# A hybrid encoder step on one Trainium2 core: the selection rounds' share of streamed work, and the engine of the first head pair's copies

## The chip, the cores and the metric

The kernel runs as one program on one core of a Trainium2 chip. The metric is the time of one execution on the device in microseconds (us); the number to predict is the median of the changed kernel's runs. A core has five engines that run unsynchronized except for semaphores: TensorE (matmuls, PE in the profile; its weight loads are PEld), VectorE (DVE), ScalarE (ACT), GpSimd (POOL) and SyncE (SP, which here mostly issues DMAs). Each engine takes its own instructions strictly in order: an instruction that waits holds up everything that stands behind it on that engine.

## The reference, cut to what matters

One layer of a streaming encoder for 1024 prompt tokens and 32 sample tokens. The normalized input `h` is projected once, and the columns are split; then come a state-space branch, a sparse attention branch, gates and an output projection.

```python
z = jnp.einsum('btd,de->bte', h, w_in)                      # h: 1056 x 1024
u, zs, q, k, v, za, qi, ki, wi, gm = jnp.split(z, offs, axis=-1)
...
logits = jnp.einsum('bthd,bsd->bths', qi, ki_all) * IDX_DIM ** -0.5
score = jnp.einsum('bth,bths->bts', wi, jax.nn.relu(logits))  # per query and key
score = jnp.where(adm[None, None, :], score, -jnp.inf)
top_val, top_idx = lax.top_k(score, n_sel)                    # 256 keys per query (136 for the sample)
kg, vg = gather(k_all, top_idx), gather(v_all, top_idx)
p = jax.nn.softmax(jnp.einsum('bthd,btkhd->bthk', q, kg) * HEAD_DIM ** -0.5)
o = jnp.einsum('bthk,btkhd->bthd', p, vg)                     # 8 heads of 64
```

Keys and values are outputs too, with one row per token (`k_p`, `v_p` for the prompt, `k_s`, `v_s` for the sample).

## The kernel before, in words

**Precision and tiles.** Each fp32 product is three TensorE matmuls of a high and a low part (`mm3`, lines 272 to 274: high by high, high by low, low by high). Activations stand transposed, 128 channels by 1056 tokens, in three chunks of 352 tokens.

**The stream.** All projections are `Job`s of 128 output columns in one queue `Z` (class `Stream`). A job has three chunks (0, 1, 2), a chunk eight steps, a step one `mm3`, so three matmuls of 352 columns. The stream is written into the program between other work: `run(us)` emits as many steps as `us` divided by 0.483 (with the rest carried over as credit), and `Z.after(us, f)` emits `f` that many steps later. A chunk's evacuation from PSUM is emitted `Z.lag` behind its last step; in the selection the lag is `LAG`, 4.0. So the numbers given to `run` do not wait for anything: they decide only where in each engine's order the instructions stand.

**PSUM in the selection.** Of each job, chunks 0 and 1 are the halves of one wide tile (tag `s`, named `pss` in the profile, two buffers) and chunk 2 has a narrow one (tag `z`, named `pz`, two buffers). Transposes go to `pt`, two buffers as well.

**The selection.** For each query the 256 largest scores are found by bisection of a threshold, one bit in each of 32 rounds (the loop over `b`, here called round 0 to 31). In a round VectorE counts three score tiles (line 1552), ScalarE counts four others (line 1550), then VectorE compares the counts and sets the next threshold for both (lines 1608, 1615, 1601). Between the counts and the comparison stands `run(RS)`: the round's share of the stream. In the stretch the stream holds the jobs K0, V0, Q0 (keys, values, queries of the first pair of heads), the merge gates g7 to g15, and za0 to za3. The gates' evacuation is a tanh on ScalarE (line 707). After the rounds VectorE marks the selected keys (`mark`), and the stream goes on by `run` with other shares until za3 is done. Then comes the attention, whose items alternate with steps of the stream.

**What K0 and V0 need.** `Heads(p, heng, eng)` builds the jobs of head pair `p`; `heng` splits their weights, and `eng` makes these copies: the three evacuations of K (line 1300) and of V (line 1304) into `zf`, and in `tok_major`, after transposes on TensorE, three copies into the token-major tile `tm` (line 1258 twice, four token blocks each; line 1261 once, the last 32 rows). `tm` has one buffer for keys and values together:

```python
tm = ap_.tile([128, 9, 128], F32, name="tm", bufs=1)
...
if b < 2:
    cp(eng)(tm[:, 4 * b:4 * b + 4].rearrange("p k c -> p (k c)"), pt)
    Z.after(TW if wide[0] else TK, lambda: part(b + 1))
else:
    cp(eng)(tm[:32, 8], pt[:32, 0:128])
    sp.dma_start(outp, tm[:, 0:8])
    sp.dma_start(outs, tm[:32, 8])
```

Pairs 1 to 3 (`HD[1:]`) are built with ScalarE as `eng`; their copies stand in the attention.

**Orders.** Inside `manual_schedule` each engine's order is the order of the program text as it is emitted; nothing is reordered later on VectorE and ScalarE there, nor on TensorE.

Of the kernel before, what the change touches and what calls it, by code (L numbers as in the profile page):

```python
# [36 lines left out]
TF, TK, TW = 1.5, 1.0, 4.5  # L37
FI = 0.0006
KA, LA = 5.0, 1.0
LAG, RS, MS, RM, RB = 4.0, 4.0, 0.008, 14.0, 1  # L40
FA, FF, SW, SA, SB = ((2.0, 1.3), (2.0, 1.3), (2.4, 1.6), (1.5, 1.5)), 0.08, 1.2, 4.0, 1.0
YR = 3.9, 2.0, 2.0, 8.0, 3.0
MR, ML, YS, YW, HI, HG, JO, SF = (), 1, 10, 15, 0, 0, 8, (2, 2, 2, 1)
# [16 lines left out]
def body(nc, tc, I, O, dbg=None):  # L60
# [3 lines left out]
    te, ve, se, ge, sp = nc.tensor, nc.vector, nc.scalar, nc.gpsimd, nc.sync  # L64
# [257 lines left out]
    now, ve = ve, Later(ve, todo)  # L322
# [190 lines left out]
    ve = now  # L513
# [753 lines left out]

    def khead(X, e, leng, gap=0, then=None):
        kH, kL = (ap_.tile([128, T], F32R, name=f"{n}{e}", bufs=1) for n in ("kH", "kL"))
        X.kH[e], X.kL[e] = kH, kL  # L1270

        def load(b):
            c = slice(512 * b, 512 * b + 512)
            kd = ap_.tile([128, 512], F32, name="kd", bufs=1)
            for hf_ in range(2):
                sp.dma_start(kd[64 * hf_:64 * hf_ + 64], X.kd[64 * e:64 * e + 64, c])

            def parts():
                split(kH[:, c], kL[:, c], kd, ve, leng)
                if b == 0:  # L1280
                    load(1)
                elif then:
                    then()
            if gap:
                Z.after(gap, parts)
            else:
                parts()
        load(0)
# [120 lines left out]

    def attention(p, X):  # L1410

# [19 lines left out]
        class Sample(Soft):  # L1431
            e, i = -1, 4

            def scores(self):
                self.products(64, 544, mb8, X.qsm.rearrange("p e q -> p (e q)"), (X.kall,))

# [10 lines left out]
            def out(self):  # L1447
                po = ps_x("po", 1)
                for k in range(5):
                    n = 128 if k < 4 else 32  # L1450
                    te.matmul(po[:, 0:64], X.cvt[:, k] if k < 4 else X.vts, self.PS[:n, k], start=k == 0, stop=k == 4)
                for e in range(2):
# [101 lines left out]

    wide[0] = True
    Z.lag = LAG
    X = Heads(0, ge, ve)

    def q0_end():
        Z.after(1.0, lambda: X.values(0))  # L1560
# [355 lines left out]
```

## Time and profile before

| | us |
|---|---|
| median of the runs | 1037.23 |
| lowest of the runs | 1037.08 |
| the profiled execution | 1032.88 |
| its span, first to last instruction | 1031.1 |
| outside the span | 1.78 |
| TensorE busy | 984.4 |
| VectorE busy | 765.8 |
| ScalarE busy | 530.8 |
| GpSimd busy | 232.2 |

The profiled execution is one of its own, 4.35 us under the median. All rows come from it, with times from the start of the span. Busy time counts instructions that compute; waiting and issuing of DMAs do not count. TensorE's matmuls are pipelined, so the rows of two of them overlap; a step's three matmuls start 0.48 us apart from the next step's.

### The profile page before, as it was taken

To read this page: it belongs to the slowest core of one execution; us is meant where nothing else is said; L and a number is where in the kernel's file an instruction comes from. 1 tells how busy PE (TensorE), PEld (TensorE's weight loads), DVE (VectorE), ACT (ScalarE), POOL (GpSimd) and SP (SyncE) were. 2 spreads that over 40 slices of the span, in tenths; PEclk is the share of its full clock that TensorE was granted. 3 is DMA by queue.
4 is the path that set the end of the run, shared out by engine and by line. 5 is a ranking of instruction groups with operands and counts; after the bars stand their busy time and mean duration, and the time that the engine had idled before them with its cause. 6 is when DMAs were issued, how large, how long until landed. Compare 5 with 4: busy or idle time off the path is not lost.

```text
span 1031.1 us, 17149 instructions
## 1 busy us (share of the span) xinstructions
PE 984.4 (95%) x6194; PEld 920.7 (89%) x6194; DVE 765.8 (74%) x1760; ACT 530.8 (51%) x1153; POOL 232.2 (23%) x459
## 2 busy tenths in 40 slices
PE   5999999999999999899999999999999999999997
PEld 3799999999998889899899999889998988998786
DVE  4669798996857879999999556667558776785544
ACT  3642245546545665778883356465466554343111
POOL 3102400000010023242333523324412222430000
PEclk9999999999999999999999999999999999999999
DMA  9922522327672213333222522232226523753311
GB/s 306 283 74 84 162 68 65 96 74 242 196 222 83 62 31 94 94 93 95 83 84 85 171 90 63 73 94 63 97 59 192 161 76 113 247 167 122 133 62 62
DMA packets 124177, 121.68 MB, mean 118 GB/s; under 512 B 14272, under 2 KB 104852, under 8 KB 124092
## 3 DMA queue, kind: packets, MB, share of 16 engines
q1 hardware_dynamic: 122544, 119.69, 37.6%
q8 instruction: 49, 0.80, 0.3%
q10 hardware_dynamic: 1388, 0.86, 0.3%
q14 instruction: 36, 0.29, 0.1%
q0 software_dynamic: 160, 0.03, 0.0%
HBM read 85.64 MB, written 34.34 MB: 116 GB/s over the span
## 4 chain that ended last, share of the span: by engine, by line
PE 77%; DVE 10%; ACT 6%; issue 3%; DMA 3%; SPq 0%; POOL 0%; POOLq 0%; ACTq 0%; DVEq 0%
PE pz L272 12%; PE pz L273 12%; PE pz L274 12%; PE pss L272 3%; PE pss L274 3%; PE pss L273 3%; DVE junk L1552 3%; PE pss L1386 3%; PE psm L1885 3%; PE psm L1886 3%; PE psm L1887 3%; DMA wm<-in_w_mod 2%; PE pt L1479 2%; PE pspo L1498 2%; PE pss L1215 2%
## 5 line engine op out<-in xcount | busy, mean ns | idle before, releaser
L272 PE MATMUL pz<-hH,wh 128*128 128x352 f32 (+1 forms) x776 | 260.5, 336 | 0.4 <-DVE qis L1060 0.4
L274 PE MATMUL pz<-hH,wl 128*128 128x352 f32 (+1 forms) x776 | 250.7, 323 | 0.0
L273 PE MATMUL pz<-hL,wh 128*128 128x352 f32 (+1 forms) x776 | 250.6, 323 | 0.0
L265 POOL TENSOR_TENSOR wl<-raw,wh 128x256 fp32r<-128x256 f32 (+1 forms) x184 | 130.9, 739 | 111.6 <-ACT wh L260 111.3
L272 PEld LDWEIGHTS pz<-hH,wh 128*128 128x128 f32 (+1 forms) x776 | 145.2, 187 | 4.0 <-issue 0.8
L273 PEld LDWEIGHTS pz<-hL,wh 128*128 128x128 f32 (+1 forms) x776 | 145.3, 187 | 1.5
L274 PEld LDWEIGHTS pz<-hH,wl 128*128 128x128 f32 (+1 forms) x776 | 145.0, 187 | 0.4
L1550 ACT ACTIVATE junkb<-sco,thr 128x768 bf16<-128x768 f32 (+3 forms) x128 | 96.8, 756 | 36.6 <-DVE thr L1615 26.6
L1552 DVE TENSOR_SCALAR_CACHE_REDUCE junk<-sco,thr 128x1024 bf16<-128x1024 f32 (+2 forms) x96 | 105.4, 1098 | 2.2
L272 PE MATMUL pss<-hH,wh 128*128 128x352 f32 x304 | 101.5, 334 | 5.8 <-POOL wh L264 3.2
L273 PE MATMUL pss<-hL,wh 128*128 128x352 f32 x304 | 99.8, 328 | 0.2 <-DVE hL L74 0.2
L274 PE MATMUL pss<-hH,wl 128*128 128x352 f32 x304 | 99.7, 328 | 0.0
L264 POOL CAST wh<-raw 128x256 fp32r<-128x256 f32 x92 | 36.2, 433 | 189.0 <-PE pz L273 178.1
L1482 DVE TENSOR_TENSOR PL<-pt,PH 128x512 fp32r<-128x512 f32 (+2 forms) x96 | 50.3, 552 | 25.8 <-ACT PH L1481 22.9
L1481 ACT CAST PH<-pt 128x512 fp32r<-128x512 f32 (+2 forms) x96 | 42.9, 482 | 46.3 <-PE pt L1479 44.5
L272 PEld LDWEIGHTS pss<-hH,wh 128*128 128x128 f32 x304 | 58.6, 193 | 8.9 <-POOL wh L264 4.9
L273 PEld LDWEIGHTS pss<-hL,wh 128*128 128x128 f32 x304 | 58.5, 192 | 0.5 <-DVE hL L74 0.4
L274 PEld LDWEIGHTS pss<-hH,wl 128*128 128x128 f32 x304 | 58.4, 192 | 0.2 <-POOL wl L265 0.2
L1223 DVE SCALAR_TENSOR_TENSOR sco<-rl,wi,sco 128x384 f32<-128x384 f32 (+6 forms) x49 | 45.5, 936 | 16.9 <-ACT rl L1218 16.3
L1218 ACT ACTIVATE rl<-pss 128x384 f32<-128x384 f32 (+6 forms) x56 | 41.2, 738 | 31.8 <-PE pss L1216 30.2
L1399 ACT ACTIVATE Sm<-Sm,mx 128x128 f32<-128x128 f32 (+8 forms) x68 | 52.7, 775 | 8.0 <-DVE mx L1392 7.3
L1392 DVE CUSTOM_DVE_ANT_0 Sm<-pss,mb 128x512 f32<-128x512 f32 (+4 forms) x68 | 40.2, 591 | 22.0 <-PE pss L1386 21.3
(408 smaller groups left out, 2210.2 us busy)
## 6 DMA issues: line engine op xcount, KB each, us to landing
raw<-in_w_in SPq DMA_DIRECT2D x44, 512.0 KB
thD<-tg SPq DMA_DIRECT2D x16, 528.0 KB
tgl<-thD SPq DMA_DIRECT2D x16, 528.0 KB
wm<-in_w_mod SPq DMA_DIRECT2D x8, 1024.0 KB
rraw<-in_w_mod SPq DMA_DIRECT2D x4, 1024.0 KB
kd<-kd SPq DMA_DIRECT2D x32, 128.0 KB
xo<-in_x_prompt SPq DMA_DIRECT2D x8, 512.0 KB
rawo<-in_w_o SPq DMA_DIRECT2D x8, 512.0 KB
```

The lines of the kernel that those rows point to most:

```text
L265: leng.tensor_sub(wl[:, c], raw[:, c], f32(wh[:, c]))
L272: te.matmul(ps, wh, xh, start=first, stop=False)
L273: te.matmul(ps, wh, xl, start=False, stop=False)
L274: te.matmul(ps, wl, xh, start=False, stop=last)
L1218: se.activation(rl[:m, :nk], ps[:m, :nk], AF.Relu)
L1223: ve.scalar_tensor_tensor(sco[i][:m, :nk], rl[:m, :nk], w, sco[i][:m, :nk], op0=ALU.mult, op1=ALU.add)
L1392: ve.tensor_tensor_reduce(self.P[:m, c], S, self.mask[:m, c], -0.125, 3.0e38 if a == 0 else mx[:m, 0:1], op0=ALU.add, op1=ALU.min, accum_o ...
L1399: se.activation(P, P, AF.Exp, scale=-1.0, bias=self.mx, accum_out=self.rs)
L1481: se.copy(PH[:, b0:b1_, oc], src)
L1482: ve.tensor_sub(PL[:, b0:b1_, oc], src, f32(PH[:, b0:b1_, oc]))
L1550: se.activation(junkb[:m, :nk], x[:m], AF.Sign, bias=t, accum_out=cnt[:m, k:k + 1])
L1552: ve.tensor_scalar(junk[:m, :nk], x[:m], t, None, op0=ALU.is_lt, op1=ALU.add, accum_out=cnt[:m, k:k + 1])
```

## The change

Two constants change. `RS`, the share of the stream that each of the 32 rounds hands out, goes from 4.0 to 4.1. The first head pair is built with ScalarE (`se`) in place of VectorE (`ve`) as `eng`, so its six evacuations and six token-major copies go to ScalarE.

```diff
-LAG, RS, MS, RM, RB = 4.0, 4.0, 0.008, 14.0, 1
+LAG, RS, MS, RM, RB = 4.0, 4.1, 0.008, 14.0, 1
...
     wide[0] = True
     Z.lag = LAG
-    X = Heads(0, ge, ve)
+    X = Heads(0, ge, se)
```

On ScalarE, rounds 5 to 7 of the selection (the four rows of line 1550 are one round's counts; `zf` is an evacuation, `tm` the token-major tile, `kall` the sample's keys). The difference, before (-) and after (+):

```order
+L1258 COPY tm<-pt 128x512
+L1304 COPY zf<-pss 128x352
+L1550 ACTIVATE junkb,cnt<-sco_3235,thr 128x768
+L1550 ACTIVATE junkb,cnt<-sco_3233,thr 128x512
+L1550 ACTIVATE junkb,cnt<-sco_3232,thr 128x384
+L1550 ACTIVATE junkb,cnt<-sco_3238,thr 32x544
+L1261 COPY tm<-pt 32x128
 L1338 COPY kall<-zf 128x32
+L1304 COPY zf<-pz 128x352
+L1258 COPY tm<-pt 128x512
 L1550 ACTIVATE junkb,cnt<-sco_3235,thr 128x768
```

Round 5 ends with K's second token copy and V's evacuation, round 6 with K's last 32 rows, the small key copy, V's last evacuation and V's first token copy; the last row shown is the first count of round 7. On VectorE V's first token copy stood in round 7.

On ScalarE, rounds 7 to 9, at the query casts (`qs`):

```order
 L1550 ACTIVATE junkb,cnt<-sco_3232,thr 128x384
 L1550 ACTIVATE junkb,cnt<-sco_3238,thr 32x544
+L1258 COPY tm<-pt 128x512
 L1316 CAST qs_4509<-pss 64x352
 L1316 CAST qs_4510<-pss 64x352
```

In round 8 V's second token copy stands ahead of the two casts; in round 9 its last 32 rows do in the same way.

On ScalarE, round 14, the evacuations of gate job g8 (`tg` out of `pss` is chunk 0 or 1, out of `pz` chunk 2):

```order
 L707 ACTIVATE tg<-pss 128x352
+L707 ACTIVATE tg<-pz 128x352
+L1550 ACTIVATE junkb,cnt<-sco_3235,thr 128x768
+L1550 ACTIVATE junkb,cnt<-sco_3233,thr 128x512
+L1550 ACTIVATE junkb,cnt<-sco_3232,thr 128x384
+L1550 ACTIVATE junkb,cnt<-sco_3238,thr 32x544
```

Chunk 2 now follows chunk 1 in the same round; before, a round's counts stood between them. Counted through the whole order, the rounds that hold the evacuation of chunk 1 are, before: g7 11, g8 14, g9 17, g10 20, g11 23, g12 25, g13 28, g14 31; after: 11, 14, 16, 19, 22, 25, 28, 30. On TensorE no instruction of the selection changes its place.

On TensorE, one of the places in the attention (`Sm` are softmax rows being transposed):

```order
 L274 MATMUL pz<-hH_81,wl 128x352
-L272 MATMUL pz<-hH_749,wh 128x352
-L273 MATMUL pz<-hL_750,wh 128x352
-L274 MATMUL pz<-hH_749,wl 128x352
 L1479 MATMUL pt<-idf,Sm 128x128 x2
+L272 MATMUL pz<-hH_749,wh 128x352
+L273 MATMUL pz<-hL_750,wh 128x352
+L274 MATMUL pz<-hH_749,wl 128x352
```

One step of the stream has moved from before two transposes to behind them.

## Rows read from the trace of the kernel before

**Rows 1.** Stretch, length, then busy us of PE, PEld, DVE, ACT, POOL (instructions).

```profile
385.00:540.00 155.00, 146.67 (x898) 144.17 (x891) 146.79 (x331) 117.37 (x282) 52.44 (x99) 0.98 0.30 92
...
586.00:870.00 284.00, 271.90 (x1816) 254.18 (x1816) 187.18 (x543) 162.57 (x377) 85.91 (x181) 1.00 0.32 97
```

**Rows 2.** Timeline of TensorE: start, duration, instruction, idle before it and releaser.

```profile
419.58 0.65 PE L1343 MATMUL pt<-idf,ckt 128*128 128x128 f32 x4 [0.49 <-DVE tm L1261]
424.39 0.75 PE L1256 MATMUL pt<-idf,zf 128*128 128x128 f32 x4 [2.22 <-DVE tm L1258]
...
464.64 0.40 PE L272 MATMUL pss<-hH,wh 128*128 128x352 f32 x1 [2.38 <-ACT tg L707]
479.04 0.40 PE L272 MATMUL pss<-hH,wh 128*128 128x352 f32 x1 [1.10 <-POOL wh L264]
...
504.70 0.40 PE L272 MATMUL pss<-hH,wh 128*128 128x352 f32 x1 [1.10 <-POOL wh L264]
...
527.82 0.32 PE L272 MATMUL pss<-hH,wh 128*128 128x352 f32 x1
```

**Rows 3.** Granted TensorE clock (before the last two numbers) behind the long spells.

```profile
424.75:428.25 3.50, 3.50 (x15) 3.50 (x14) 3.33 (x8) 2.44 (x6) 1.56 (x5) 0.51 0.00 0
466.00:469.00 3.00, 3.00 (x12) 3.00 (x11) 2.90 (x6) 1.84 (x5) 0.98 (x2) 0.50 0.51 133
```

**Rows 4.** Timeline of ScalarE: first counts of rounds 1, 7, 11, 12; evacuations; copies.

```profile
392.32 0.94 ACT L1550 ACTIVATE junkb<-sco,thr 128x768 bf16<-128x768 f32 x1 [5.83 <-DVE thr L1613]
...
420.32 0.94 ACT L1550 ACTIVATE junkb<-sco,thr 128x768 bf16<-128x768 f32 x1 [0.80 <-DVE thr L1615]
...
445.79 0.94 ACT L1550 ACTIVATE junkb<-sco,thr 128x768 bf16<-128x768 f32 x1 [2.17 <-DVE thr L1615]
...
449.20 0.44 ACT L707 ACTIVATE tg<-pss 128x352 f32<-128x352 f32 x1
449.78 0.94 ACT L1550 ACTIVATE junkb<-sco,thr 128x768 bf16<-128x768 f32 x1
...
478.46 0.44 ACT L707 ACTIVATE tg<-pss 128x352 f32<-128x352 f32 x1
...
525.78 0.44 ACT L707 ACTIVATE tg<-pss 128x352 f32<-128x352 f32 x1
...
610.72 0.58 ACT L1258 COPY tm<-pt 128x512 f32<-128x512 f32 x1
611.19 0.47 ACT L1304 COPY zf<-pz 128x352 f32<-128x352 f32 x1
```

**Rows 5.** Timeline of VectorE: threshold instructions of round 2, copies, waits.

```profile
400.42 0.48 DVE L1608 TENSOR_TENSOR keep<-cnt,lim 128x7 int32<-128x7 f32 x1
400.94 0.66 DVE L1615 SCALAR_TENSOR_TENSOR thr<-keep,nxt 128x7 int32<-128x7 int32 x1
...
409.24 0.68 DVE L1258 COPY tm<-pt 128x512 f32<-128x512 f32 x1
409.84 0.51 DVE L1304 COPY zf<-pss 128x352 f32<-128x352 f32 x1
...
419.25 0.28 DVE L1261 COPY tm<-pt 32x128 f32<-32x128 f32 x1
...
430.53 1.06 DVE L1320 TENSOR_TENSOR qs<-pss,qs 64x352 fp32r<-64x352 f32 x2 [0.18 <-ACT qs L1316]
...
470.82 0.17 DVE L1615 SCALAR_TENSOR_TENSOR thr<-keep,nxt 128x7 int32<-128x7 int32 x1
...
586.04 0.29 DVE L1392 CUSTOM_DVE_ANT_0 Sm<-pss,mb 128x128 f32<-128x128 f32 x1 [5.83 <-PE pss L1386]
```

**Rows 6.** Timeline of SyncE: K's rest, za3's 528 KB store, the load that waits for it.

```profile
419.55 0.35 SPq L1263 DMA_DIRECT2D out_k_s<-tm  x1
...
586.36 0.32 SPq L698 DMA_DIRECT2D zaD<-zt  x1
589.56 0.32 SPq L1417 DMA_DIRECT2D ya<-zaD  x1
```

## The prediction, made before the changed kernel ran

> **What bounds the kernel now.** I read the stretches first, then TensorE's idle spells, then what releases them. In the two stretches that the change touches (the selection from 385 to 540 us, the attention from 586 to 870) TensorE is busy 146.67 of 155.00 and 271.90 of 284.00 us [rows 1]; between them it does not idle at all. So only what TensorE waits for can be won. In the selection it idles six times: 0.49, 2.22, 2.38 us and three spells of 1.1 us, two of which are shown; 8.4 in all [rows 2]. After the two long ones its granted clock falls to 0.5, the lower of its two levels, for nearly all of a 3.5 us and a 3.0 us stretch [rows 3], which costs some 1.7 us each. All that could be gained here is therefore 8.4 + 3.4 = 11.8 us, 1.1%.
>
> What holds TensorE in those spells? The three of 1.1 us are put down to GpSimd's weight cast. But the spell that ends at 479.04 ends 0.14 us after ScalarE's tanh of 478.46 + 0.44 [rows 2, 4]. That fits the code: chunks 0 and 1 of a job share one of two wide PSUM tiles, so job j may start only when chunk 1 of job j-2 is evacuated, and ScalarE does that behind the counts of the round in which the planner put it. **TensorE's speed limit in the selection is the pace of the rounds**, not its own work. Two jobs without idle take 527.82 - 504.70 = 23.12 us, 11.56 each [rows 2]; three rounds take longer. The binding event near the end is the evacuation at 525.78 + 0.44 + 0.14 = 526.36, in round 28 (the first of the 32 is round 0), which job g15 waits for; it started at 527.82 [rows 2, 4]. From there to the attention nothing stops TensorE, and VectorE then waits 5.83 us for it [rows 5]. So I need one number: **how far does round 28 move?** If it ends d later, TensorE gains 527.82 - 526.36 - d = 1.46 - d us, provided that no wait remains behind it.
>
> **RS = 4.1.** A round hands out 8.49 steps instead of 8.28. TensorE's own order in the selection does not change; what changes is the round in which ScalarE finds an evacuation. The order shows g8's chunks 1 and 2 together in round 14, where g12's two stood in round 25 before. Chunk 1 of g9, g10, g11 and g14 is thus evacuated one round earlier (rounds 16, 19, 22, 30), some 4 us, which frees the three spells of 1.1 us. Chunk 1 of g8, g12 and g13 stays in rounds 14, 25 and 28. So TensorE runs ahead after g10, gains, and meets the wall again at round 25 (g14) and round 28 (g15). This is why the 3.2 us of extra quota (32 x 0.1) do not appear as such: the sum stops at 1.46 - d.
>
> **Twelve copies from VectorE to ScalarE.** Off VectorE go six evacuations of 0.51 us, four copies of 0.68 and two of 0.28 [rows 5], 6.3 us of instruction time, about 5.4 by the distance of their starts. But a round without a copy on VectorE is not VectorE's: from 445.79 to 449.78 ScalarE's counts fill 3.41 us, its tanh 0.44, and the next counts start 3.99 us after the first [rows 4]. ScalarE has 0.14 us of room. I lay out its rounds from 392.32, where round 1 starts [rows 4]:
> - rounds 1 and 3, counts and one evacuation: 3.99 each.
> - rounds 2 and 5: the same or slightly more on ScalarE, but GpSimd's weight split lies over the end of the round. In round 2 it stretched the two short threshold instructions to 0.48 and 0.66 us from 0.17 [rows 5], so 0.8 more: 4.79 each.
> - round 4: token copy and evacuation start 0.47 apart [rows 4], 3.41 + 0.47 + 0.47 = 4.35.
> - Round 6 starts at 392.32 + 21.91 = 414.23. It holds four copies: K's 32-row rest, the small key copy, V's last evacuation, and V's first token copy, which the order puts one round earlier than before.
>
> Here the change **adds a wait**. V's token tile is K's token tile (one buffer), so V's first copy must wait until K's rest has been stored to HBM, and that store is issued only after the rest is copied, in the same round. Before, the store went out at 419.55 [rows 6] and a whole set of counts lay in between. Now the rest is copied at 414.23 + 3.41 to 417.9, the store goes out, and ScalarE stands; behind V's copy in its queue are the counts of round 7, and behind those VectorE's threshold. No row shows this landing. From below it is hidden: the four copies alone give 3.41 + 0.2 + 0.12 + 0.36 + 0.59 = 4.68 us (the first three read from overlaps like those of rows 4, an estimate), so round 7 at 418.9. From above it is the 528 KB store of 586.36, whose reader was let go at 589.56 [rows 6], 3.2 us: round 7 at 417.9 + 3.2 + 0.6 = 421.7. The store is 16 KB, so nearly none of that time is data, but it cannot be nothing; I take the middle, 1.6 us: 420.1 against 420.32 before [rows 4]. So the whole relief of rounds 1 to 6 shrinks to 0.2 us.
>
> The Trainium skill (DMA: Bandwidth & Descriptors, Anatomy of one DMA) gives a transfer a fixed 2.0 us, most of it the receipt of the write; its fit is for GpSimd's path, this store goes by SyncE. By it round 7 would start at 420.5 and the gain at the end would be 0.4 us smaller. No run here shows the landing yet.
>
> Rounds 8 and 9: V's next copies stand ahead of the query casts. VectorE waits for both casts (it idled 0.18 us for them at 430.53, behind its own copy [rows 5]), so 0.47 and 0.20 us come onto the path; in round 7 the copy that leaves was inside such a wait and saves nothing. The value and key splits that move between rounds 9 to 12 keep their sum. So d = -0.2 + 0.47 + 0.20 = **0.5 us later**, and it stays to round 28 (the round with two evacuations costs the same in round 14 as in 25).
>
> **TensorE's early spells.** The 0.49 and 2.22 us waits for VectorE's token copies go: V's first copy is done by 420.1, and TensorE asks for that buffer at 424.39 - 2.22 - 0.49 = 421.7 [rows 2]. With the slow stretch behind them that is 4.4 us, but it is given back: job g9 would arrive at 462.26 - 11.56 - 4.4 = 446.3, and its PSUM tile comes free with round 11's evacuation at 449.20 + 0.44 + 0.14 + 0.5 = 450.3 [rows 2, 4]. I expect a new spell of about 4 us there, one of 1 to 2 us before g10 (round 14), none before g11 to g13, and about 1 us before g14 and g15.
>
> **Attention.** The stream enters it with another fraction of a step, so at some 40 places one step of three matmuls (0.48 us) stands on the other side of a transpose, score or product. TensorE idles 12.1 us there now [rows 1], in spells of 0.2 to 1.6 us. Both directions occur; I take 0, bounds -1.5 and +1.5.
>
> **Sum.** 1.46 - 0.5 = 1.0 us faster. Against the profiled execution, 1032.88 - 1.0 = 1031.9; it lies 4.35 us under the median, so the median becomes 1037.23 - 1.0 = **1036.2 us**. With the ends of the unknown landing, d runs from -0.7 (hidden) to +2.1 (3.2 us): 1035.1 to 1037.9; with the attention's 1.5, 1033.6 to 1039.4.
>
> **Rivals.**
> 1. *The relief counts in full.* If ScalarE has room (its copies overlap its counts, the landing is hidden) rounds end by the 5.4 us earlier that VectorE loses. For it: VectorE is busy 146.79 of 155.00 us and ScalarE 117.37 [rows 1]. Against it: the 0.14 us of room. Round 28 is then at 521.0, g15 starts there, gain 1.46 + 5.4 = 6.9: 1030.4.
> 2. *ScalarE becomes the bound, slower than before.* The landing takes the full 3.2 us, and V's value splits, now both in round 9, meet GpSimd's split for another 0.8: d = 2.1 + 0.8 = 2.9, loss 1.4: 1038.7. It decides from d = 1.46 on. For it: all the moved copies stand in ScalarE's queue in front of counts that VectorE's next threshold needs. Against it: a 16 KB store.
> 3. *The quota counts as it says*: 3.2 us more work under the rounds. That would need the wall of rounds 25 and 28 not to bind, for instance if TensorE arrives there late; then the three spells of 1.1 us and the clock stretch after 464.64 fall away, 3.2 + 1.7 = 4.9: 1032.3. Against it: g13's evacuation keeps its round.
> 4. *The attention's shifted steps* outweigh all, by 2 us or more in either direction: 1034 or 1039.
>
> **Chances.** Forecast 0.55, first rival 0.12, second 0.17, third 0.08, fourth 0.08. The range 1031.5 to 1039.5 leaves out the first rival and the outer parts of the second and fourth. About 2% (21 us) is what a measurement of this kernel tells from no change; no case comes near it: faster 0.01, same 0.98, slower 0.01.
>
> **What would show it.** In the changed profile: ScalarE idle before V's first token copy in round 6, released by a transfer; round 7 at about 420; round 11's tanh near 449.6; no idle of TensorE before 440, then a spell near 450 that ends with that tanh, a slow clock stretch after it, no spells of 1.1 us after g10; g15 at about 526.9; the scores of the attention 1 us earlier, with VectorE still waiting there. Wrong would be the whole if a round without copies on VectorE got shorter than 3.99 us, if ScalarE did not stand in round 6, or if TensorE's spells in the attention changed by more than 1.5 us.

## The result, and the profile after

The changed kernel takes 1028.94 us where the kernel before took 1035.71 in the same series (medians of 6 runs each): a ratio of 0.9945, 95% interval 0.9925 to 0.9966. One of the six runs of the kernel before, 1212.29 us, counts in its median but not in the ratio; the other five have a median of 1034.34 us. Timed once more beside three of the experiments the ratio was 0.9966 (0.9953 to 0.9979). Both intervals hold 0.9953 to 0.9966, a gain of 3.5 to 4.9 us. I had forecast a gain of 1.0 us, and a time of 1036.2 us in a range from 1031.5 to 1039.5; 1028.94 lies below it.

The profiled executions took 1032.88 us before and 1029.09 after. The windows of the changed kernel, with the columns of [rows 1]; the second one begins 0.6 us behind the attention's first scores, that of [rows 1] 0.3 us:

```profile
385.00:540.00 155.00, 147.85 (x911) 145.32 (x904) 140.50 (x320) 123.25 (x297) 52.32 (x99) 0.98 0.32 95
584.00:868.00 284.00, 274.33 (x1828) 255.65 (x1827) 187.16 (x544) 163.24 (x378) 85.48 (x180) 1.00 0.32 100
```

TensorE is 1.2 us busier in the selection and 2.4 us busier in the attention. The gain has two places, then, and the sum had put a small one in the first and nothing in the second.

TensorE's timeline after, the four waits of the selection and the attention's first scores (they answer to [rows 2]):

```profile
451.93 0.63 PE L272 MATMUL pss<-hH,wh 128*128 128x352 f32 x1 [5.54 <-ACT tg L707]
...
501.08 0.40 PE L272 MATMUL pss<-hH,wh 128*128 128x352 f32 x1 [0.50 <-ACT tg L707]
...
513.45 0.40 PE L272 MATMUL pss<-hH,wh 128*128 128x352 f32 x1 [0.59 <-ACT tg L707]
...
525.72 0.40 PE L272 MATMUL pss<-hH,wh 128*128 128x352 f32 x1 [0.51 <-ACT tg L707]
...
583.40 0.22 PE L1386 MATMUL pss<-kH,qs 128*128 128x128 f32 x1
```

The six spells have become one long one, where the prediction put it, and three of half a microsecond, all of which end with a tanh of ScalarE. Job g15 starts at 525.72 instead of 527.82. The tanh that frees it, in round 28, and the one that ends the long spell, in round 11:

```profile
451.35 0.44 ACT L707 ACTIVATE tg<-pss 128x352 f32<-128x352 f32 x1
...
525.14 0.44 ACT L707 ACTIVATE tg<-pss 128x352 f32<-128x352 f32 x1
```

525.14 + 0.44 + 0.14 = 525.72, to the digit. Behind the long spell the granted clock (third number from the end) is at its lower level for some four microseconds, as after the long spells of [rows 3]:

```profile
452.00:456.00 4.00, 4.00 (x14) 4.00 (x15) 3.86 (x9) 2.95 (x7) 0.00 (x0) 0.50 0.42 103
456.00:460.00 4.00, 4.00 (x25) 4.00 (x24) 3.74 (x10) 3.75 (x10) 0.00 (x0) 0.92 0.65 229
```

The wait that the change adds is there too. ScalarE in round 6, and the first count of round 7 (compare [rows 4]):

```profile
417.69 0.24 ACT L1261 COPY tm<-pt 32x128 f32<-32x128 f32 x1
417.84 0.21 ACT L1338 COPY kall<-zf 128x32 f32<-128x32 f32 x1
417.96 0.44 ACT L1304 COPY zf<-pz 128x352 f32<-128x352 f32 x1
420.95 0.59 ACT L1258 COPY tm<-pt 128x512 f32<-128x512 f32 x1 [2.55 <-DMA out_k_s<-tm]
421.43 0.94 ACT L1550 ACTIVATE junkb<-sco,thr 128x768 bf16<-128x768 f32 x1
```

The store that it waits for, on SyncE:

```profile
417.96 0.34 SPq L1263 DMA_DIRECT2D out_k_s<-tm  x1
```

It was issued at 417.96, and its tile was free at 420.95: 2.99 us.

**Where the rounds made it up.** I measure from round 1 (392.32 before, 392.49 after). Round 7 is 0.94 us later than before, round 9 1.77, round 15 0.28 *earlier*, round 28 0.82 earlier. So 2.05 us come back from round 9 to round 15 and 0.54 after that. In the kernel before, rounds 12 and 14, with the second and the fourth of the first pair's key splits (lines 73 and 74), read so on VectorE:

```profile
453.11 0.64 DVE L73 CAST kH<-kd 128x512 fp32r<-128x512 f32 x1
453.78 1.11 DVE L74 TENSOR_TENSOR kL<-kd,kH 128x512 fp32r<-128x512 f32 x1
454.82 0.69 DVE L1608 TENSOR_TENSOR keep<-cnt,lim 128x7 int32<-128x7 f32 x1
...
463.99 0.57 DVE L73 CAST kH<-kd 128x512 fp32r<-128x512 f32 x1
464.60 1.10 DVE L74 TENSOR_TENSOR kL<-kd,kH 128x512 fp32r<-128x512 f32 x1
465.62 0.70 DVE L1608 TENSOR_TENSOR keep<-cnt,lim 128x7 int32<-128x7 f32 x1
466.35 0.65 DVE L1615 SCALAR_TENSOR_TENSOR thr<-keep,nxt 128x7 int32<-128x7 int32 x1
```

and GpSimd beside them, in the kernel before, splits weights:

```profile
452.04 3.45 POOL L265 TENSOR_TENSOR wl<-raw,wh 128x256 fp32r<-128x256 f32 x4
...
463.56 3.42 POOL L265 TENSOR_TENSOR wl<-raw,wh 128x256 fp32r<-128x256 f32 x4
```

The same two key splits of the changed kernel, the second now in round 11, the fourth still in round 14, and then its GpSimd with the two weight splits around them:

```profile
451.43 0.42 DVE L73 CAST kH<-kd 128x512 fp32r<-128x512 f32 x1
451.89 0.69 DVE L74 TENSOR_TENSOR kL<-kd,kH 128x512 fp32r<-128x512 f32 x1
452.50 0.16 DVE L1608 TENSOR_TENSOR keep<-cnt,lim 128x7 int32<-128x7 f32 x1
...
465.12 0.42 DVE L73 CAST kH<-kd 128x512 fp32r<-128x512 f32 x1
465.58 0.69 DVE L74 TENSOR_TENSOR kL<-kd,kH 128x512 fp32r<-128x512 f32 x1
466.19 0.36 DVE L1608 TENSOR_TENSOR keep<-cnt,lim 128x7 int32<-128x7 f32 x1
466.58 0.31 DVE L1615 SCALAR_TENSOR_TENSOR thr<-keep,nxt 128x7 int32<-128x7 int32 x1
```

```profile
448.16 2.78 POOL L265 TENSOR_TENSOR wl<-raw,wh 128x256 fp32r<-128x256 f32 x4
465.75 1.82 POOL L264 CAST wh<-raw 128x256 fp32r<-128x256 f32 x4 [14.80 <-PE pz L273]
```

A split of weights may start when the job two places ahead of it has ended and left its buffers. Job g8 now ends earlier, since TensorE's early waits are gone, and g9 later, since it waits 5.54 us to start; so one split moved ahead of these key splits and the next mostly behind them. The second key split also stands one round earlier in VectorE's order, but that alone would not have freed it: counted from round 1, the two key splits now start at 58.9 and 72.6 us, and GpSimd's weight splits of the kernel before lay at 58.3 to 63.2 and 69.8 to 74.7 us. I added up by how much VectorE's instructions in rounds 9 to 14 exceed what they take beside an idle GpSimd: 3.2 us before, 1.2 after, and the difference is what came back there. Whether this is the cause, and not only what stands beside it, the experiments must tell.

### The profile page after: what moved, and what is told of

Read it like the earlier page. It is cut to its first block, busy times and chain, and to the rows that moved or that the text cites. A ratio compares the mean times of both kernels' runs of the same rounds, so it can differ in the third digit from the quotient of the medians.

```text
span 1027.3 us, 17151 instructions
## 1 busy us (share of the span) xinstructions
PE 984.7 (96%) x6194; PEld 920.5 (90%) x6194; DVE 759.5 (74%) x1748; ACT 536.3 (52%) x1165; POOL 232.1 (23%) x459
## 4 chain that ended last, share of the span: by engine, by line
PE 71%; DVE 11%; ACT 10%; issue 3%; DMA 3%; POOL 0%; SPq 0%; ACTq 0%; POOLq 0%; DVEq 0%
PE pz L272 12%; PE pz L273 11%; PE pz L274 11%; ACT junkb L1550 6%; DVE junk L1552 3%; PE pss L1386 3%; PE psm L1885 3%; PE psm L1886 3%; PE psm L1887 3%; DMA wm<-in_w_mod 2%; PE pt L1479 2%; PE pss L272 2%; PE pss L273 2%; PE pss L274 2%; PE pspo L1498 2%
## 5 line engine op out<-in xcount | busy, mean ns | idle before, releaser
L265 POOL TENSOR_TENSOR wl<-raw,wh 128x256 fp32r<-128x256 f32 (+1 forms) x184 | 128.4, 725 | 117.3 <-ACT wh L260 117.0
```

Of the source, the lines that this page charges most:

```text
L265: leng.tensor_sub(wl[:, c], raw[:, c], f32(wh[:, c]))
```

## The experiments

All ratios are to the kernel before on the same chip. **My theory**: the gain is the sum of two effects that the change does not name: the moved weight splits of GpSimd (some 2 us), and another order of steps in the attention (some 2 us). **The rivals**: the relief of VectorE as such; the quota as such.

| kernel | ratio (95%) | round 1 | first scores | end | round 1 to scores | scores to end |
|---|---|---|---|---|---|---|
| before | 1 | 392.32 | 585.66 | 1031.1 | 193.34 | 445.4 |
| changed | 0.9945 (0.9925 to 0.9966) | 392.49 | 583.40 | 1027.3 | 190.91 | 443.9 |
| after_again | 0.9966 (0.9953 to 0.9979) | 391.80 | 582.36 | 1026.3 | 190.56 | 443.9 |
| quota_alone | 0.9971 (0.9954 to 0.9988) | 392.43 | 584.18 | 1027.4 | 191.75 | 443.2 |
| scalar_alone | 1.0003 (0.9992 to 1.0014) | 393.23 | 585.55 | 1030.9 | 192.32 | 445.4 |
| both_old_fraction | 0.9981 (0.9967 to 0.9994) | 395.69 | 586.55 | 1032.0 | 190.86 | 445.4 |
| before_new_fraction | 0.9978 (0.9965 to 0.9992) | 392.65 | 586.20 | 1029.4 | 193.55 | 443.2 |
| before_no_splits | 0.998 (0.997 to 0.999) | 395.52 | 585.60 | 1031.0 | 190.08 | 445.4 |
| after_two_splits_more | 0.9996 (0.9985 to 1.0008) | 394.60 | 588.84 | 1032.6 | 194.24 | 443.8 |
| after_own_v_tile | 0.9949 (0.9936 to 0.9962) | 392.33 | 582.15 | 1025.7 | 189.82 | 443.6 |
| after_other_fraction | 1.0015 (1.0005 to 1.0025) | 392.98 | 584.35 | 1033.6 | 191.37 | 449.2 |
| own_v_tile_no_splits | 0.9899 (0.9879 to 0.992) | 391.63 | 576.68 | 1020.7 | 185.05 | 444.0 |
| quota_own_v_tile | 0.996 (0.9946 to 0.9975) | 395.89 | 586.49 | 1030.6 | 190.60 | 444.1 |
| own_v_tile_third_fraction | 0.9943 (0.9926 to 0.9959) | 394.18 | 584.23 | 1027.6 | 190.05 | 443.4 |
| own_v_tile_small_pieces | 0.9984 (0.9972 to 0.9995) | 394.75 | 588.39 | 1032.0 | 193.64 | 443.6 |
| own_v_tile_large_pieces | 0.9997 (0.9984 to 1.001) | 392.94 | 585.70 | 1029.3 | 192.76 | 443.6 |

The last two columns are worked out from the three before them, each from one profiled execution. They are the better measure of the parts, since the time up to round 1 differs from one execution to the next.

### The two halves of the diff

**quota_alone** takes RS = 4.1 alone, **scalar_alone** the twelve copies alone.

```diff
-    X = Heads(0, ge, se)
+    X = Heads(0, ge, ve)      # quota_alone, in the changed kernel
-    X = Heads(0, ge, ve)
+    X = Heads(0, ge, se)      # scalar_alone, in the kernel before
```

> Only RS = 4.1; the first heads' copies stay on VectorE. TensorE's order is that of the changed kernel, its attention included. Theory (my reading of the two traces): about 2 us of the gain come from the selection, where TensorE's long wait before g9 moved GpSimd's weight split off the two rounds (12 and 14) in which it stretched VectorE's key splits, so that the rounds made up the time they had lost; about 2 us come from the attention, whose steps of the stream stand on other sides of its transposes and scores. Here the waits of 0.49 and 2.22 us stay and nothing is moved off rounds 12 and 14, so round 28 ends where it did and g15 gains 0.5 to 1.5 us, the attention 2: 2.5 to 3.5 us faster, 1032.2 to 1033.2 against 1035.7. Rival 'the quota is all': the full 5.7 us, 1030. Rival 'ScalarE's relief is all': nothing, 1035.7.

> Only the twelve copies go to ScalarE; RS = 4.0. TensorE's order is that of the kernel before everywhere. Theory: the attention gains nothing; the early waits of TensorE go, a long one stands near g9 or g10, the weight split moves, and g15 starts 0 to 1 us earlier: 1034.7 to 1035.7. Rival 'the relief is all': 5 to 6 us faster, 1030. Rival 'ScalarE pays': 1 us slower, 1036.7, since V's first token copy waits 3 us for the store of K's rest and no quota makes up for it.

The copies alone have no gain that can be measured, so the rival that credits VectorE's relief falls, and with it the first rival of the prediction (5.4 us of relief). The quota alone cannot be told from the whole change: 0.9971 lies in the interval of the changed kernel's second timing, and from round 1 to the end its trace takes 635.0 us, those of the changed kernel 634.8 and 634.5, that of the kernel before 638.8. Both effects of my theory come with the quota, then; that the copies add anything to it is not shown.

My expectation for the quota fitted in size and was wrong on the way. I had TensorE's 2.22 us wait for V's token copy stay and nothing move off rounds 12 and 14. But the wait shrank to 0.84 us, a spell of 4.86 us came before g9, GpSimd's weight splits moved as in the changed kernel, and VectorE's excess in rounds 9 to 14 was 1.0 us.

The added wait shows where it comes from. With the quota alone, VectorE stands for the same store:

```profile
422.37 0.69 DVE L1258 COPY tm<-pt 128x512 f32<-128x512 f32 x1 [2.31 <-DMA out_k_s<-tm]
```

With the copies on ScalarE and RS = 4.0 nothing waits there: V's first copy stands one round later. So the wait belongs to the quota, not to the engine. For scalar_alone the trace shows a selection shorter by 1.0 us, which its timing does not confirm. It also shows where the relief goes: round 28 comes 1.8 us earlier than before, but with RS = 4.0 the evacuation that g13 waits for stands in round 23, and 504.25 + 0.44 + 0.14 = 504.83 is where g13 starts, only 0.8 us earlier than before counted from round 1; behind it TensorE has no wait left to lose. GpSimd's splits moved here as well, but they met others of VectorE's instructions, and the excess in rounds 9 to 14 stayed at 3.2 us.

### The attention by itself

The stream enters the attention with a fraction of a step: 0.472 in the kernel before, 0.097 in the changed one. **both_old_fraction** and **before_new_fraction** exchange the two, **after_other_fraction** takes a third.

```diff
     Z.flush()
+    Z.credit = 0.4720   # both_old_fraction; 0.0973 in before_new_fraction, 0.75 in after_other_fraction
     Z.lag = 0
```

> The changed kernel, but at the entry of the attention the stream's credit is set to the fraction 0.472 that the kernel before has there (the changed one has 0.097): TensorE's order is then that of the kernel before over the whole program, and only the selection's change is left. Theory: the selection's 2 us remain, 1033.7. Rival 'the attention gives nothing': as the changed kernel, 1029 to 1030.

> The kernel before, with the fraction 0.097 of the changed kernel set at the entry of the attention: nothing of the change in the selection, all of it in the attention. Theory: 2 us faster, 1033.7. Rival 'the attention gives nothing': 1035.7. By a third reading, in which the attention is what the selection was not, all 5.7: 1030.

> The changed kernel, with the stream's fraction at the entry of the attention set to 0.75 (0.097 in the changed kernel, 0.472 in that before): the selection is the changed kernel's, the order in the attention a third one. Theory: the attention's time depends on which side of a transpose or score a step falls, not on the amount of work, so the third order gives another time between 2 us less and 3 us more than the changed kernel's. Rival 'a small fraction is better as such': at 0.75 at least as slow as at 0.472, 2 us or more over the changed kernel.

This parts the gain cleanly. The selection alone gives 0.9981, the fraction alone 0.9978. From the first scores to the end it is 445.4 us in all four kernels with the old fraction and 443.2 to 444.1 in all with the changed one, whatever stands ahead. What TensorE waited for from 584 to 880 us, total, times and the longest, in the kernel before:

```profile
PE pspo L1498 <- DVE PL L1482: 2.6, 4, 0.7
...
PE pt L1343 <- DVE PL L1482: 1.8, 3, 0.9
PE pss L1386 <- DVE mx L1392: 1.6, 1, 1.6
```

and in before_new_fraction:

```profile
PE pspo L1498 <- DVE PL L1482: 0.9, 2, 0.7
PE pt L1343 <- DVE PL L1482: 0.9, 3, 0.4
PE pss L1386 <- DVE mx L1392: 0.5, 2, 0.2
```

In all, TensorE waits 9.0 us instead of 12.1 in the 284 us behind the first scores; another of its waits (`pz` for VectorE's `m`) rose from 2.8 to 3.9 us. I read it so that a step of the stream that stands ahead of such an instruction fills its wait; no run moves one step by itself. The third fraction costs 3.8 us more than the old one, beyond the bounds that I gave it (up to 3 over the changed kernel, 5.3 measured). A fourth, below, gave 443.4 us at 0.25, where 0.097 gave 443.2 to 444.1. So the time is level up to 0.25 and longer at 0.472 and 0.75; whether a larger fraction is worse as such or each order has a time of its own, four values do not decide.

### GpSimd's weight splits: taken away, and put back

**before_no_splits** takes two weight splits out of the kernel before; two gates are computed with other weights. **after_two_splits_more** puts GpSimd work beside two key splits of the changed kernel.

```diff
             if j < len(self.jobs) and j not in self.parts:
                 b = self.jobs[j]
                 self.load(j)
+                if b.name in ('g10', 'g11'):      # before_no_splits
+                    self.parts[j] = self.parts[j - 1]
+                    return
                 self.parts[j] = wparts(self.raw[j], b.kt, b.n, heng=b.heng, leng=b.leng)
...
                 split(kH[:, c], kL[:, c], kd, ve, leng)
+                if X.p == 0 and b != e:           # after_two_splits_more
+                    scr = ap_.tile([128, 512], F32, name="scr", bufs=1)
+                    for q in range(2):
+                        ge.tensor_sub(scr, f32(kH[:, c]), f32(kH[:, c]))
```

> The kernel before, but GpSimd makes no weight split for the jobs g10 and g11: both take g9's split weights, so two of the gates are computed with other weights than the reference's; TensorE, VectorE and ScalarE have the same instructions in the same order. GpSimd is then still from about 443 to 478 us, in rounds 12 and 14, whose key splits took VectorE 1.11 us and whose threshold instructions 0.65 to 0.70 us where others take 0.69 and 0.17. Theory (GpSimd's split is what these rounds lose): they become 1.2 and 1.6 us shorter (6.03 to 4.8, 6.43 to 4.85), the locks of TensorE behind them come 2.7 us earlier, and the attention's first scores start 193.34 - 2.5 us after round 1: 2.5 us faster than before, about 0.9976. Rival 'the early waits of TensorE are what the change won', with GpSimd a bystander: nothing, 1.000.

> The changed kernel, with GpSimd work put where it had been moved away: beside the second key split of the first head and the first of the second head GpSimd makes two subtractions of 128x512 into a scratch tile that nobody reads (it starts when VectorE's cast of the split is done; nothing waits for it). The other engines keep their order. Theory: each of the two rounds becomes 1.2 to 1.4 us longer, so the rounds do not make up what they lose in round 6; round 28 ends 2.4 to 2.8 us later, g15 starts as late as in the kernel before, and only the attention's 2 us are left of the gain: ratio to before 0.998, 2.5 us slower than the changed kernel. Rival: as the changed kernel, 0.995 to 0.996.

Without the two splits the kernel before, unchanged on every other engine, wins 3.3 us in the trace of its selection and some 2 in its timing (0.998). Not all went as laid out: the split of g12 moved ahead into round 12, whose length stayed, and round 14 alone lost 1.58 us of the 2.8 there; the rest came in rounds 15 to 27, which took 53.16 us instead of 55.29. Round 28 so came 3.7 us earlier, of which TensorE got the 3.3. The converse is as clear. Round 11 of after_two_splits_more with GpSimd's added work:

```profile
454.07 0.69 DVE L74 TENSOR_TENSOR kL<-kd,kH 128x512 fp32r<-128x512 f32 x1
454.68 1.00 DVE L1612 TENSOR_TENSOR keep<-cnt,lim 128x7 int32<-128x7 f32 x1
455.71 0.17 DVE L1619 SCALAR_TENSOR_TENSOR thr<-keep,nxt 128x7 int32<-128x7 int32 x1
455.92 0.90 DVE L1605 TENSOR_SCALAR nxt<-thr 128x7 int32<-128x7 int32 x1
```

```profile
454.11 2.68 POOL L1283 TENSOR_TENSOR scr<-kH 128x512 f32<-128x512 f32 x2 [0.99 <-DVE kH L73]
```

Round 28 comes 3.3 us later than in the changed kernel, g15 starts as much later, and the ratio is back at 0.9996. Nothing waits for the added work but through VectorE's short instructions. It cost 3.3 us where I had 2.4 to 2.8: round 14 met the split of g11 as well.

### V's own token tile, and the limit

**after_own_v_tile** removes the added wait. **own_v_tile_no_splits** also leaves out the weight splits of g8 to g15 (all take g7's, so eight gates are computed with other weights). **quota_own_v_tile** has the tile without ScalarE's copies, **own_v_tile_third_fraction** the tile and the fraction 0.25. **after_again** is the changed kernel.

```diff
-        tm = ap_.tile([128, 9, 128], F32, name="tm", bufs=1)
+        if wide[0] and name == "v":
+            tm = ap_.tile([128, 9, 128], F32, name="tmv", bufs=1)
+        else:
+            tm = ap_.tile([128, 9, 128], F32, name="tm", bufs=1)
...
+                if b.name in [f'g{f}' for f in range(8, 16)]:     # own_v_tile_no_splits
+                    self.parts[j] = self.parts[j - 1]
+                    return
```

> The changed kernel, with a token tile of V's own for the first pair, so that V's first copy does not wait for the store of K's last rows. Order of every engine unchanged. Theory: ScalarE's idle 2.55 us in round 6 falls away, rounds 7 to 28 start about 2.5 us earlier unless GpSimd's split of g11 (when g9 ends) moves on to round 14's key split, which gives 1.3 us back; g15 is held by round 28 and starts 1.2 to 2.5 us earlier: 1.2 to 2.5 us faster than the changed kernel, ratio to before 0.992 to 0.994. Rival 'the added wait is hidden, TensorE is held elsewhere': as the changed kernel.

> The changed kernel itself, beside the three that follow on one chip, to narrow its ratio (0.9925 to 0.9966). By the sum of the parts measured one at a time (selection 0.9981, attention 0.9978; in the traces 2.4 us and 1.5 to 2.2 us): 0.9955 to 0.9962. By the first timing alone: 0.9945.

> The changed kernel with V's own token tile, and GpSimd makes no weight split for g8 to g15: all take g7's split weights, so eight gates are computed with other weights than the reference's; the other engines keep their instructions and their order. It measures what GpSimd's splits cost the rounds. Theory: the stretch of VectorE's threshold and key split instructions, 7.0 us in the selection with V's own tile, falls to the 2 to 3 us of the splits ahead of g8; the rounds gain 4 us, TensorE's four spells (4.4, 0.7, 0.4, 0.7) shrink to one of at most 4, and the first scores come 2 to 4 us earlier than with V's own tile alone: ratio 0.991 to 0.993. Rival 'the stretch is not on the path': as V's own tile alone, 0.995.

> RS = 4.1 and V's own token tile; the twelve copies stay on VectorE. By the runs so far: the quota alone had the same wait for the store of K's rest (its round 6 took 7.40 us), so it should gain the same 1 us from the own tile as the changed kernel did: 4 us faster than before, 0.996, as the changed kernel. Rival 'ScalarE's copies are worth something by themselves': 0.9970.

> The changed kernel with V's own token tile and the fraction 0.25 at the entry of the attention. Traces so far from the first scores to the end: 443.2 to 443.9 us at 0.097, 445.4 at 0.472, 449.2 at 0.75. If the time grows with the fraction, 444 to 445 here and a ratio of 0.995 to 0.996; if each order has its own time, anything from 442 to 449.

The wait is gone in after_own_v_tile: ScalarE copies at 418.34 and starts round 7 at 418.81. But the selection gains only 1.1 us against the changed kernel (0.7 against after_again), under the 1.2 to 2.5 expected: round 7 took 6.92 us instead of 6.24 and round 9 9.37 instead of 8.66, so over half of the 2.5 us that round 7 had gained was given back; in both rounds it was VectorE beside GpSimd that took longer. The timing cannot tell it from the changed kernel, nor own_v_tile_third_fraction, which at 0.9943 has the lowest ratio of the kernels that compute everything. quota_own_v_tile came as expected, with a selection 1.2 us shorter than quota_alone's and 0.996; its interval still holds the 0.9970 of the rival.

Without the splits the selection is 4.8 us shorter than with V's own tile alone. VectorE's threshold and key split instructions from 391 to 540 us, busy time and mean ns, in after_own_v_tile:

```profile
L1618 DVE SCALAR_TENSOR_TENSOR thr<-keep,nxt 128x7 int32<-128x7 int32 x31 | 7.7, 249 | 1.1
L1604 DVE TENSOR_SCALAR nxt<-thr 128x7 int32<-128x7 int32 x30 | 7.4, 246 | 1.0
L1611 DVE TENSOR_TENSOR keep<-cnt,lim 128x7 int32<-128x7 f32 x31 | 7.4, 238 | 3.3 <-ACT tg L707 0.5 <-ACT junkb L1553 0.3
L74 DVE TENSOR_TENSOR kL<-kd,kH 128x512 fp32r<-128x512 f32 x4 | 2.8, 692 | 0.1
```

and in own_v_tile_no_splits:

```profile
L1614 DVE TENSOR_TENSOR keep<-cnt,lim 128x7 int32<-128x7 f32 x31 | 5.9, 192 | 4.0 <-ACT junkb L1556 0.8 <-ACT tg L710 0.5
L1621 DVE SCALAR_TENSOR_TENSOR thr<-keep,nxt 128x7 int32<-128x7 int32 x31 | 5.6, 182 | 1.1
L1607 DVE TENSOR_SCALAR nxt<-thr 128x7 int32<-128x7 int32 x30 | 5.6, 187 | 1.0
L74 DVE TENSOR_TENSOR kL<-kd,kH 128x512 fp32r<-128x512 f32 x4 | 2.8, 692 | 0.1
```

25.3 against 19.9 us, for the same instructions on the same sizes. TensorE's four spells became two, of 2.33 and 1.92 us. The gain was over what I expected (0.9899, not 0.991 to 0.993). The rival, that the stretch is off the path, falls.

### How the stretch comes about

**own_v_tile_small_pieces** and **own_v_tile_large_pieces** cut GpSimd's splits into eight and two pieces instead of four.

```diff
         pc = kt // 4 if ge in (heng, leng) and kt % 4 == 0 else kt
+        if wide[0] and pc < kt:
+            pc = kt // 8      # small; kt // 2 in large
```

> The changed kernel with V's own token tile; in the selection GpSimd splits a job's weights in eight pieces of 128x128 instead of four of 128x256 (the same elements; cast and subtraction in pieces of half the size). The other engines keep their order. Theory 'VectorE's threshold and key split instructions wait until GpSimd's present instruction has ended': each wait is half as long, their stretch in the selection falls from 7.0 us to about 3.5 to 4, and the first scores come 1.5 to 3 us earlier, 187 to 188.3 us after round 1 instead of 189.8; ratio to before 0.992 to 0.9935. Rival 'the two engines share the bandwidth while both run': the stretch stays about 7 us, the ratio 0.995.

> As the run before it, but with two pieces of 128x512. Theory: each wait is up to twice as long, the stretch grows to 10 to 14 us, the first scores come 2 to 5 us later than with four pieces; ratio to before 0.997 to 1.000. Rival: no change, 0.995.

The single instruction answers clearly. A held threshold instruction, 0.17 us elsewhere, of the small pieces:

```profile
402.53 0.38 DVE L1620 SCALAR_TENSOR_TENSOR thr<-keep,nxt 128x7 int32<-128x7 int32 x1
```

and of the large pieces:

```profile
424.42 1.22 DVE L1620 SCALAR_TENSOR_TENSOR thr<-keep,nxt 128x7 int32<-128x7 int32 x1
425.67 1.23 DVE L1606 TENSOR_SCALAR nxt<-thr 128x7 int32<-128x7 int32 x1
```

Four pieces had 0.66 in [rows 5]. GpSimd's subtractions last 0.47, 0.74 and 1.31 us on average with eight, four and two pieces, so the hold grows with the single instruction, as it does if it lasts until the present one ends. Not every hold was that short: of the comparisons (`keep`) of the small pieces, three took 0.70, 0.93 and 1.16 us, over two or three of GpSimd's pieces. Shared bandwidth, the rival, would have left it alike. The Trainium skill (SBUF — State Buffer, SBUF: two separate sides) describes such a hold: VectorE, where it reads two SBUF inputs or runs in a two-port mode, and GpSimd take a shared port pair by an exclusive lock for a whole instruction, and the other blocks. The rows agree for the instructions with two inputs, and for VectorE's counts, which stay at a mean of 1.27, 1.15 and 0.88 us before and after. The casts and the threshold instruction `nxt<-thr` are held with one input; whether they run in a two-port mode no row shows.

The sum did not follow for the small pieces: I expected the holds of the selection to halve and to give 1.5 to 3 us, and the selection became 3.8 us longer. The means of lines 1620 and 1606 did fall, from 249 and 246 ns to 207 and 209, but that of the comparison rose from 238 to 283. Up to round 9 the small pieces were 1.9 us ahead of the four; round 9 then took 11.74 us instead of 9.37. VectorE and then GpSimd of the small pieces:

```profile
439.77 3.43 DVE L1374 CAST V<-tmv 128x512 fp32r<-128x512 f32 x1
```

```profile
439.96 2.96 POOL L267 TENSOR_TENSOR wl<-raw,wh 128x128 fp32r<-128x128 f32 x7
```

A cast of 0.42 us was held through seven instructions in a row. GpSimd also needed 66.9 us instead of 51.6 for the same elements. By the start of g15 the small pieces were 1.7 us behind the four; the other 2.1 us came behind the rounds, where TensorE stood 0.85 us at 555.70 and 0.28 at 556.73 for GpSimd's `wl`. How much of the loss each of these causes makes up I have not measured apart. The large pieces went the expected way, 2.9 us longer than four.

## Why the prediction was wrong

**TensorE's tie to the rounds was right.** "TensorE gains 1.46 - d" holds: with d = -0.82 it gives 2.28, and g15 started 133.23 us after round 1 instead of 135.50, 2.27 earlier. The long spell, its end with round 11's tanh, the slow clock behind it and ScalarE's stand in round 6 came as laid out, each one to two microseconds later: the spell was 5.54 us, not 4, and ended at 451.93, not 450.3. None came before g10, where I had 1 to 2 us, and g13 to g15 wait half a microsecond each, where I had about 1 for the last two.

**The landing was mis-sized.** I took 1.6 us; the copy ran 2.99 us after the issue (2.72 in after_again, from 417.47 to 420.19), near my upper bound of 3.2. In the six traces that have this wait it is 2.71 to 3.06 us. The 2.0 us that I quoted from the Trainium skill (DMA: Bandwidth & Descriptors, Anatomy of one DMA) is for another path, and all six lie above it. By itself this should have made the change worse: round 7 came at 421.43, not 420.1.

**The step that failed is "d = 0.5 us later, and it stays to round 28"**, with the sentence ahead of it that the key splits of rounds 9 to 12 keep their sum. Up to round 9 the delay was even larger (1.77 us). Then rounds 9 to 14 gave 2.05 us back and the later ones 0.54, so that d was not +0.5 but -0.82. I had priced GpSimd's weight split where it stood over round 2 (0.8 us), and treated it as fixed to the rounds. But it follows TensorE: it starts when a job's buffers come free. A change that moves TensorE by some microseconds moves each later split against the rounds, and each meeting costs some 0.5 us an instruction. The splits taken away and put back show GpSimd's splits as the cause, and the excess of rounds 9 to 14 (3.2 us before, 1.2 after) has the size; [rows 5] had the price.

**The attention was mis-sized**: I took 0 with bounds of 1.5, and the exchange of the fractions measured 1.5 to 2.2 us in the traces, 0.9978 in time. TensorE's busy time there rose by 2.4 us, over the 1.5 that the prediction had named as a sign of being wrong. The direction could not be read from the order by what I did, which was to count places and not to ask which wait each step would fill.

**The rivals.** The first (relief in full) is refuted by scalar_alone. The third (the quota as it says, 4.9) names the half of the change that has the gain, but not its mechanism: g13's evacuation kept its round, and of quota_alone's gain 2.2 us stand behind the first scores and only 1.6 in the selection. The second had its first condition nearly met, a landing of 2.99 us, and at round 10 the delay was 2.87 us, as large as its 2.9; but the value splits in round 9 lost only 0.1 us to GpSimd, and by round 28 the delay was gone. The fourth, an attention that moves by 2 us or more, was about half of what happened.

**The base.** 1037.23 was the median of three runs, one of them the 1212.29 us; the kernel before had 1033.5 to 1035.7 in all later series, so the predicted time was 1.5 to 3.8 us too high for that reason alone. Between the two profiled executions the gain is 3.8 us: 2.4 in the selection, 1.5 behind the first scores, less 0.2 ahead of round 1.

## What to carry to other kernels

When an engine far off the critical path runs on an event of the bound engine, ask where its work will fall after the change: a hold of half a microsecond weighs most on a chain of short instructions (here 0.17 us became 0.66). Lay out a delay only as far as the next place where such work meets the chain; behind it the delay is not conserved. And where a planner carries a remainder from one phase into the next, time the phases apart, with the remainder set by hand, before crediting a change with what it does in the second.

## What the hardware showed that I had not expected

- One cast of VectorE was held 3.0 us through seven back-to-back GpSimd instructions, and was not let in between them (the rows above), while most threshold instructions were let in after one, and some of the small pieces' comparisons only after two or three.
- Halving GpSimd's instructions from 128x256 to 128x128 cost it 66.9 instead of 51.6 us of busy time for the same elements in the stretch of 155 us.
- The way to round 1 took 391.63 to 395.89 us in the sixteen profiled executions, though the kernels differ only from the selection on, some 7 us ahead of round 1 at the earliest. Such a spread is as large as the whole gain, so I compared traces from round 1 on.
